# Attention's output differences in a tile of their own, and head 1's recurrence a few slots later

## The chip, the cores and the metric

The kernel runs on one core of one Trainium2 chip. The metric is device time in microseconds (us): the median of several runs of the whole program. Five engines with queues of their own work beside each other: TensorE (PE, matmuls), VectorE (DVE), ScalarE (ACT), GpSimd (POOL) and SyncE (SP, which here only issues DMA transfers). Each engine and each issuing queue works in order: an entry that waits holds up everything behind it on the same queue.

## The reference

One step of an encoder layer over 512 prompt and 32 sample frames with 2048 features, in float32. Heads of a gated recurrence (HGRN2) and heads of latent attention (MLA) run beside each other, their outputs are joined and projected, and a convolutional FFN follows:

```python
proj = x @ w_in
hq, hf, hi, hg, cq, ckv, kr = jnp.split(proj, SPLITS, axis=-1)
f = lb + (1.0 - lb) * jax.nn.sigmoid(hf)
o_h, s_new = hgrn2_recurrence(heads(hq), heads(1.0 - f), heads(jnp.log(f)), heads(hi), s0, blk)
...
o_a = mla_attention(q_nope, q_rope, k_nope, krs, v, q_pos, jnp.arange(past_len + T))
out = jnp.concatenate([o_h, o_a.reshape(B, T, D_MLA)], axis=-1) @ w_out
...
h = layer_norm(ALPHA * h + mix, ln1_g, ln1_b)
ff, conv_new = conv_ffn(h, conv_cache, w_up, w_gate, conv_w, conv_b, w_down)
h = layer_norm(ALPHA * h + ff, ln2_g, ln2_b)
```

There are 8 recurrent heads and 8 attention heads. `NI` is half of the 544 frames, 272.

## The kernel before

Each float32 operand is split into a high part (a copy by ACT, `wh`, `aH`) and a low part (a subtraction by DVE, `wl`, `aL`), and each product is made of three matmuls.

Most of the large projections are done by a divided product that needs 7 block products in place of 8. It works on sums and differences of the weight's four quarters and of the activations' quarters. `sums_of_inputs` forms these sums of the normalised input early and stores them in device memory (`si_dr`), using tiles of the attention's pool `mp` as rooms (the list `homes`). The sums come back as operands: s1 and s2 into a pool of their own (`smr`), s4 at the start of the next stage (`load_sum(gp, "s4")`, two loads at L738), s3 into the low halves of input tiles (`place_s3`, L781).

Sums of the later output projection's weights are formed by transfers alone: the list `forms` holds 32 of them (L93). The first 8 are issued by SP during the first projections. The other 24 are issued by POOL, two at a time, from `low` each time a divided product prepares its "s2" weights (L835). Groups c = 2 to 15 of divided products exist, two for each head from head 1 on. Stage 3 of the kernel, from about 767 us, reads the result.

Attention works on pairs of heads (`proj_pair`, `attend`). `attend(pr)` takes 9 items (query blocks). For each it makes scores, a softmax into a tile `p` (three slots, taken in turn, L603), transposes, and a product with the values, copied into the output tile `o` (L655, L651). At the end `o` is stored to `cat_dr` (L670), the difference of its two halves of frames is formed in place (L671, on POOL for pairs 0 to 2 and on DVE for pair 3), and the difference is stored to `d3_dr` (L672). Pair 3 runs beside the projection `head_ig(0)`, whose last step on DVE (L398) reads a PSUM tile that the next product needs.

The next stage opens the pool `gp` in the place of `mp`; a transfer into a `gp` tile waits for the last readers of whatever lay there. On PE, DVE and ACT its order is written out by hand, in slots. A divided group has 7 products in the order 11, s1, s2, s4, s3, 12, 22; each product has 24 matmuls (L889) and two slots, so a group has 14 slots and a head 28. At the middle of each product the result of the product before is taken out of PSUM (L874, L877), the weights of the product two further on get their low part (L831), and sums of raw weights are formed (L818, and L820 and L833 as adding transfers on POOL). Behind each slot's matmuls come steps of side work, given to slots by `beside_from(slot, generator, steps)`:

- `split_s4`: two steps, each an ACT copy (L742) and a DVE subtraction (L743) of half of s4. Its operands are first needed by the product s4, in slots 6 and 7.
- `split_s3`: four steps (L786, L787).
- `levels(h)`: the recurrence inside chunks. Step 0 makes Kp and Qp (L931, L932). Step 1 makes ten matmuls into the PSUM tile `sw` (L937), a masked copy (L938) and the first of seven levels. Each level is one set of matmuls (L954, L957, or L952 for the last) and DVE products of Qp and Kp (L958, L960), of totals (L966) and a masked copy (L970). The matmuls of a level need the products of the level before.
- `finish(h)`: 15 steps: transposes (L990), states (L1000, L1005 to L1014), outputs (L1022, L1024), their norm and gate, and the sums for the output projection, which read `cat_dr` and `d3_dr` through the tile `ab` (L983, L984).

`sw` has one buffer; the level matmuls and the state sums share two PSUM tiles in turn. Before, `levels(0)` takes slots 2 to 12, `finish(0)` 15 to 29, `levels(1)` 15 to 29, `finish(1)` 30 to 44, `levels(2)` 43 to 57. SP's and POOL's entries are put in order by a planner from the program order and its own estimate of what is ready.

Of the kernel before, what the change touches and what calls it, by code (L numbers as in the profile page):

```python
# [7 lines left out]
F32 = mybir.dt.float32  # L8
# [3 lines left out]
ALU = mybir.AluOpType  # L12
# [3 lines left out]
P = 128  # L16
# [4 lines left out]
T = TP + TS  # L21
PAST = 128
NK = TP + PAST + TS
HEADS = 8
# [18 lines left out]
NI = T // 2  # L43
# [12 lines left out]
N_PLAIN = 2  # L56
# [3 lines left out]
def tile_encoder_step(ctx, tc, xp, xs, w_in, w_in4, w_kr, w_q_b, w_kv_b, w_out, w_out4, w_up, w_gate, w_down, w_down2,  # L60
# [3 lines left out]
    V, A, G, PE = nc.vector, nc.scalar, nc.gpsimd, nc.tensor  # L64
    dma = nc.sync.dma_start
# [11 lines left out]
    d3_dr = [dram.tile([P, 2, NI], F32, name=f"d3d{k}", tag=f"d3d{k}") for k in range(HK // 2)]  # L77
# [19 lines left out]
    def form_next(n=0):  # L97
        if len(forms) > n:
            tc.keep_in_program_order(forms.pop(0)())
# [82 lines left out]
    def minus(out, a, b):  # L182
        V.tensor_tensor(out=out, in0=a, in1=b, op=ALU.subtract)

    def opposite(out, a, b):
        V.scalar_tensor_tensor(out=out, in0=a, scalar=-1.0, in1=b, op0=ALU.mult, op1=ALU.subtract)
# [215 lines left out]
    with tc.tile_pool(name="mp", bufs=1, side="right", reuse_waits="tile") as mp, tc.tile_pool(name="psa", bufs=4, space=PSUM) as psa:  # L402
# [17 lines left out]
        def a_tile():  # L420
            return psa.tile([P, 512], F32, name="at", tag="at")
# [48 lines left out]
        c = {}  # L470
# [140 lines left out]
        def attend(pr):  # L611
            qn, qr, kn, vt = pairs[pr]
            o = mp.tile([P, 2 * T], F32, name="o", tag="o").rearrange("p (j c) -> p j c", j=2)

            def scores(b, j):
                sc = a_tile()
                if b == 4:
                    for j, k in enumerate((kn[0], kn[1], krs)):
                        PE.matmul(sc[:, :160], qlast[pr % 2][:, j], k[:, TP:NK], start=j == 0, stop=j == 2)
                    return softmax(sc[:, :160], P, 160)  # L620
                nk = (b + 1) * P
                q0 = b * P
                PE.matmul(sc[:, :nk], qn[j][:, q0:q0 + P], kn[j][:, :nk], start=True, stop=False)
                for i, k in enumerate(c["kr"]):
                    PE.matmul(sc[:, :nk], qr[j][:, q0:q0 + P], k[:, :nk], start=False, stop=i == 1)
                V.tensor_tensor(out=sc[:64, q0 + 64:nk], in0=sc[:64, q0 + 64:nk], in1=amask, op=ALU.add)
                return softmax(sc[:, :nk], P, nk)

            def turn(b, p):
                tp = a_tile()  # L630
                t = mp.tile([P, T], F32, name="pT", tag="pT", bufs=3)
                if b == 4:
                    PE.transpose(tp[:, 0:P], p[:, 0:P], ident)
                    PE.transpose(tp[:, P:2 * P], p[:, 32:160], ident)
                    A.activation(plast[96:128, :], tp[96:128, P:P + 64], AF.Copy)
                    n = 64
                else:
                    n = (b + 1) * P
                    for k in range(b + 1):
                        PE.transpose(tp[:, k * P:(k + 1) * P], p[:, k * P:(k + 1) * P], ident)  # L640
                A.activation(t[:, :n], tp[:, :n], AF.Copy)
                return t

            def values(b, j, t):
                po = a_tile()
                if b == 4:
                    for j in range(2):
                        js = slice(j * 32, (j + 1) * 32)
                        PE.matmul(po[:, js], vt[:, 4, j, :], t[:, js], start=True, stop=False)
                        PE.matmul(po[:, js], vt[:, 5, j, :], plast[:, js], start=False, stop=True)  # L650
                    V.tensor_copy(o[:, :, TP:T], po[:, :64].rearrange("p (j c) -> p j c", j=2))  # L651
                    return
                for k in range(b + 1):
                    PE.matmul(po[:, :P], vt[:, k, j, :], t[:, k * P:(k + 1) * P], start=k == 0, stop=k == b)
                V.tensor_copy(o[:, j, b * P:(b + 1) * P], po[:, :P])  # L655

            items = [(b, j) for b in range(4) for j in range(2)] + [(4, 0)]
            n = len(items)
            ps, ts_ = {}, {}
            for i in range(n + 3):  # L660
                if i < n:
                    ps[i] = scores(*items[i])
                    yield
                if 0 <= i - 2 < n:
                    ts_[i - 2] = turn(items[i - 2][0], ps.pop(i - 2))
                    yield
                if 0 <= i - 3 < n:
                    values(*items[i - 3], ts_.pop(i - 3))
                    yield
            dma(cat_dr[4 + pr], o)  # L670
            (V if pr == 3 else G).tensor_tensor(out=o[:, :, :NI], in0=o[:, :, :NI], in1=o[:, :, NI:], op=ALU.subtract)  # L671
            dma(d3_dr[pr], o[:, :, :NI])  # L672

        ticks = [0]

# [4 lines left out]

        def sums_of_inputs():
            homes = [("p", T, 3)] * 3 + [("kn", NK, 2)] * 2 + [("pT", T, 3)] * 3
            homes += [(t, n, 1) for t, n in (("o", 2 * T), ("vt", 12 * P), ("qr0", 2 * T), ("qr1", 2 * T))]

            def room():
                for tag, n, bufs in homes:
                    t = mp.tile([P, n], F32, name=tag, tag=tag, bufs=bufs)
                    for i in range(n // T):
                        yield t[:, i * T:(i + 1) * T]

            rooms = room()
            rows = []
            for k in range(HK):
                rows.append((next(rooms), next(rooms)))
                for x, kg in zip(rows[k], (k, HK + k)):
                    dma(x, h0_dr[kg])
                if k % 2:
                    yield
            for k in range(HK):
                a, b = rows[k]  # L700
                t0, t1, t0b, t1b = (x[:, h] for x in (a, b) for h in H_)
                minus(t1b, t1b, t1)
                minus(t1, t0, t1)
                opposite(t0, t1b, t0)
                opposite(t0b, t0, t0b)
                for x, n in ((a, "a"), (b, "b")):
                    G.dma_start(si_dr[n][k // 4][:, k % 4], x.rearrange("p (w c) -> p w c", w=2))
                yield
# [55 lines left out]
    with tc.tile_pool(name="gp", bufs=1, side="right", reuse_waits="tile") as gp, tc.tile_pool(name="psg", bufs=1, space=PSUM) as psg:  # L764
# [37 lines left out]
        class Divided:  # L802
# [26 lines left out]
            def low(self, wh):  # L829
                wl = wp.tile([P, 1024], R, name="wl", tag="wl")  # L830
                V.tensor_tensor(out=wl, in0=self.t(self.key), in1=wh.bitcast(F32), op=ALU.subtract)  # L831
                if self.name == "s2":
                    G.dma_start(self.t("11"), self.src("21"), accum_op=ALU.add)  # L833
                    for _ in range(2):
                        form_next()  # L835
                elif self.name not in ("11", "s1"):
                    slots.append(self.raw.pop(self.key)[0])
                    supply()
                return wh, wl
# [21 lines left out]
        def settle():  # L861
            now, later[:] = later[:], []
            for f in now:
                f()
# [202 lines left out]
        with tc.manual_schedule(engines=MANUAL):  # L1067

            turns = {}

            def beside_from(slot, gen, steps):
                for n in steps:
                    turns.setdefault(slot + n, []).append(gen)

            def split_s4():
                for i in range(2):
                    split_sum("s4", i)
                    yield

            beside_from(1, split_s4(), (0, 2))  # L1080
            beside_from(4, split_s3(range(HK)), range(4))
            beside_from(0, levels(0), (2, 3, 5, 6, 7, 8, 9, 11, 12))
            beside_from(15, finish(0), range(15))
            for h in range(1, HEADS):
                s0 = 28 * (h - 1) + 15
                beside_from(s0, levels(h), (0, 2, 4, 6, 8, 10, 12, 13, 14) if h < HEADS - 1 else (0, 1, 3, 4, 6, 8, 9, 11, 12))
                if h < HEADS - 1:
                    beside_from(s0 + 15, finish(h), range(15))
            groups = [g for h in range(1, HEADS) for g in (divided_qf(h), divided_ig(h))]
            for slot, _ in enumerate(s for g in groups for s in g):  # L1090
                for gen in turns.pop(slot, ()):
                    next(gen, None)
            for _ in range(2):
                settle()
            for slot in sorted(turns):
                for gen in turns[slot]:
                    next(gen, None)
# [831 lines left out]
    with tc.manual_schedule():  # L1929
# [253 lines left out]
        class Last:  # L2183
            g, name, time = None, "11", 3.0
# [370 lines left out]
        _, rs = nrm.row_factor(ps)  # L2555
# [131 lines left out]
```

## Time and profile before

| what | value |
|---|---|
| median of 3 runs | 2342.21 us (2341.68 to 2342.52) |
| profiled execution | 2341.88 us, span 2340.1 us |
| PE busy | 2293.4 us, 98% of the span |
| DVE / ACT / POOL busy | 1724.8 / 1099.5 / 280.6 us |
| mean granted PE clock | 0.992 |
| DMA | 481.11 MB, mean 206 GB/s |

The profile is one execution. Its page gives busy times and the costliest groups; further views give the waits of an engine (who waited for whom), the rows of an engine in order of time, busy times with the granted clock in chosen stretches, and transfers with the time from issue to landing. `[0.82 <-ACT kn L584]` behind a row means that its engine sat idle for 0.82 us before it, until ACT's instruction of line 584 was done. `x24` is a count. Times in the rows are us from the start of the span. The attention pairs run from about 155 to 298 us, the hand-ordered stage follows to about 700 us.

### The profile page before, as it was taken

The numbers are of one execution on the slowest core, as the hardware profiler recorded it, in microseconds if no ns is written. First come the engines' busy times: TensorE is split into PE (matmuls) and PEld (weight loads), VectorE is DVE, ScalarE is ACT, GpSimd is POOL, SyncE is SP. The second block draws the span as 40 slices with busy tenths as digits, with TensorE's granted clock in tenths as the row PEclk, the third lists the DMA queues.
The fourth block names the chain that finished last, engine by engine and source line by source line (L and its number), as shares of the span: only waits on it lengthen the run. The fifth ranks groups of instructions, "written<-read, shape, count | busy, mean of one in ns | idle before, by whom it ended". The sixth has DMA issues, their size and how long they took to land.

```text
span 2340.1 us, 44591 instructions
## 1 busy us (share of the span) xinstructions
PE 2293.4 (98%) x18210; PEld 2276.8 (97%) x18210; DVE 1724.8 (74%) x2392; ACT 1099.5 (47%) x1684; POOL 280.6 (12%) x354
## 2 busy tenths in 40 slices
PE   7999989999999999999999999999999999999997
PEld 7999889999999999999999999999999999999997
DVE  7655657777777878987777777777777677777766
ACT  6344533444334537665455555555555433333324
POOL 1111101111101121000010000100001111111102
PEclk9999989999999999999999999999999999999998
DMA  7832356666766746777667667676676999889832
GB/s 265 294 112 89 113 141 154 173 173 187 173 178 225 264 162 206 215 209 201 206 176 230 179 187 220 169 226 187 182 224 185 365 324 312 257 276 308 291 107 79
DMA packets 176189, 481.11 MB, mean 206 GB/s; under 512 B 15984, under 2 KB 78192, under 8 KB 168560
## 3 DMA queue, kind: packets, MB, share of 16 engines
q1 hardware_dynamic: 138928, 320.76, 39.3%
q0 software_dynamic: 37056, 157.50, 29.1%
q8 instruction: 143, 2.34, 0.4%
q14 instruction: 62, 0.51, 0.1%
HBM read 398.69 MB, written 93.57 MB: 210 GB/s over the span
## 4 chain that ended last, share of the span: by engine, by line
PE 64%; ACT 1%; DVE 1%; issue 0%; ACTq 0%; DVEq 0%
PE main L1349 22%; PE acc L1349 17%; PE main L1380 11%; PE acc L1380 7%; PE acc L148 3%; PE main L148 1%; PE main L1834 1%; PE sb L1834 1%; ACT y L2435 0%; ACT wh L1290 0%; PE main L1162 0%; ACT zb L1490 0%; PE main L1157 0%; ACT za L1490 0%; PE acc L1157 0%
## 5 line engine op out<-in xcount | busy, mean ns | idle before, releaser
L1291 DVE TENSOR_TENSOR wl<-raw,wh 128x1024 fp32r<-128x1024 f32 x371 | 456.4, 1230 | 192.4 <-ACT wh L1290 192.1
L1290 ACT ACTIVATE wh<-raw 128x1024 fp32r<-128x1024 f32 x371 | 392.2, 1059 | 410.2 <-PE main L1349 99.3
L1349 PE MATMUL main<-op,wh 128*128 128x272 f32 x1408 | 265.4, 288 | 0.0
L1349 PE MATMUL acc<-ops,wh 128*128 128x272 f32 x1344 | 254.1, 288 | 0.0
L1349 PE MATMUL main<-ops,wh 128*128 128x272 f32 x1344 | 254.1, 288 | 0.0
L1349 PEld LDWEIGHTS main<-op,wh 128*128 128x128 f32 x1408 | 221.1, 188 | 0.0
L1349 PEld LDWEIGHTS acc<-ops,wh 128*128 128x128 f32 x1344 | 211.2, 188 | 0.0
L1349 PEld LDWEIGHTS main<-ops,wh 128*128 128x128 f32 x1344 | 211.1, 188 | 0.0
L1349 PE MATMUL main<-op,wl 128*128 128x272 f32 x704 | 203.1, 289 | 0.3 <-DVE wl L1291 0.3
L1349 PE MATMUL main<-ops,wl 128*128 128x272 f32 x672 | 193.9, 289 | 0.0
L1349 PE MATMUL acc<-ops,wl 128*128 128x272 f32 x672 | 193.9, 288 | 0.0
L1349 PE MATMUL acc<-op,wh 128*128 128x272 f32 x832 | 157.5, 288 | 1.0 <-ACT ea L1675 1.0
L1290 ACT ACTIVATE wh<-rawl 128x1024 fp32r<-128x1024 f32 x93 | 98.8, 1063 | 116.7 <-PE acc L1349 39.9
L831 DVE TENSOR_TENSOR wl<-raw,wh 128x1024 fp32r<-128x1024 f32 x98 | 120.4, 1229 | 43.6 <-ACT wh L826 42.5
L889 PE MATMUL main<-s,wh 128*128 128x272 f32 x672 | 135.9, 299 | 2.5 <-DVE hproj L398 2.5
L889 PE MATMUL main<-aH,wh 128*128 128x272 f32 x448 | 133.4, 298 | 0.0
L1291 DVE TENSOR_TENSOR wl<-rawl,wh 128x1024 fp32r<-128x1024 f32 x93 | 113.8, 1224 | 26.3 <-ACT wh L1290 26.2
L1349 PEld LDWEIGHTS main<-op,wl 128*128 128x128 f32 x704 | 132.4, 188 | 0.5 <-DVE wl L1291 0.5
L1349 PEld LDWEIGHTS acc<-op,wh 128*128 128x128 f32 x832 | 130.5, 188 | 1.2 <-ACT ea L1675 1.2
L826 ACT ACTIVATE wh<-raw 128x1024 fp32r<-128x1024 f32 x98 | 103.4, 1055 | 59.4 <-DVE raw L818 58.0
L889 PE MATMUL main<-aH,wl 128*128 128x272 f32 x448 | 129.5, 289 | 0.0
L889 PE MATMUL main<-aL,wh 128*128 128x272 f32 x448 | 129.0, 288 | 0.0
(542 smaller groups left out, 6182.4 us busy)
## 6 DMA issues: line engine op xcount, KB each, us to landing
raw<-in_w_in SPq DMA_DIRECT2D x76, 512.0 KB, 5.7
raw<-in_w_up SPq DMA_DIRECT2D x71, 512.0 KB, 4.9
raw<-in_w_gate SPq DMA_DIRECT2D x71, 512.0 KB, 4.9
raw<-in_w_down SPq DMA_DIRECT2D x67, 512.0 KB, 9.2
opd<-ohl SPq DMA_DIRECT2D x20, 1088.0 KB, 5.5
ops<-opd POOLq DMA_DIRECT2D x20, 1088.0 KB, 11.9
raw<-in_w_up POOLq DMA_DIRECT2D x35, 512.0 KB, 5.2
opd<-ohl SPq DMA_DIRECT2D x20, 816.0 KB, 6.4
```

The costliest lines, as they stand in the source:

```text
L148: PE.matmul(ps, ww[:, wcols[0]:wcols[1]], aa[:, hs[j]], start=first and i == 0, stop=last and i == 2, skip_group_check=True)
L826: A.activation(wh, self.t(self.key), AF.Copy)
L831: V.tensor_tensor(out=wl, in0=self.t(self.key), in1=wh.bitcast(F32), op=ALU.subtract)
L889: PE.matmul(out, ww[:, k * P:(k + 1) * P], aa, start=name in ("11", "s1", "12") and k == 0 and q == 0, stop=k == HK - 1 and q == 2, skip_g ...
L1290: A.activation(wh, src, AF.Copy)
L1291: V.tensor_tensor(out=wl, in0=src, in1=wh.bitcast(F32), op=ALU.subtract)
L1349: PE.matmul(ps, ww[:, k * P:(k + 1) * P], aa, start=self.first and k == 0 and i == 0, stop=k == n - 1 and i == 2, skip_group_check=True)
L1380: PE.matmul(banks[:, 512 * u:512 * u + NI], ww[:, (u * n + k) * P:(u * n + k + 1) * P], aa, start=self.first and k == 0 and i == 0, stop=k ...
L1834: PE.matmul(self.bank, ww[:, k * P:(k + 1) * P], aa, start=self.first and k == 0 and i == 0, stop=k == HK - 1 and i == 2, skip_group_check ...
```

## The change

- The difference of the output's halves is written to a tile with the tag `p`, and that tile is stored; `o` is only read.
- In the list of rooms `o` comes last, so that in the pool it lies behind `vt`, `qr0` and `qr1`. The sums of inputs take their rooms in the new order.
- The first divided group (c = 2) issues no weight-sum transfer; the groups c = 3 to 14 issue the 24.
- `split_s4` has slots 3 and 4, not 1 and 3. `levels(1)` has slots 18 to 33, not 15 to 29, and `finish(1)` 34 to 48, not 30 to 44.

```diff
             dma(cat_dr[4 + pr], o)
-            (V if pr == 3 else G).tensor_tensor(out=o[:, :, :NI], in0=o[:, :, :NI], in1=o[:, :, NI:], op=ALU.subtract)
-            dma(d3_dr[pr], o[:, :, :NI])
+            d = mp.tile([P, T], F32, name="p", tag="p", bufs=3).rearrange("p (j c) -> p j c", j=2)
+            (V if pr == 3 else G).tensor_tensor(out=d, in0=o[:, :, :NI], in1=o[:, :, NI:], op=ALU.subtract)
+            dma(d3_dr[pr], d)
...
-            homes += [(t, n, 1) for t, n in (("o", 2 * T), ("vt", 12 * P), ("qr0", 2 * T), ("qr1", 2 * T))]
+            homes += [(t, n, 1) for t, n in (("vt", 12 * P), ("qr0", 2 * T), ("qr1", 2 * T), ("o", 2 * T))]
...
-                    for _ in range(2):
+                    for _ in range(2 if self.c > N_PLAIN else 0):
                         form_next()
...
-            beside_from(1, split_s4(), (0, 2))
+            beside_from(3, split_s4(), range(2))
...
                 s0 = 28 * (h - 1) + 15
-                beside_from(s0, levels(h), (0, 2, 4, 6, 8, 10, 12, 13, 14) if h < HEADS - 1 else (0, 1, 3, 4, 6, 8, 9, 11, 12))
+                beside_from(s0, levels(h), (3, 5, 7, 9, 11, 13, 15, 17, 18) if h == 1 else
+                            (0, 2, 4, 6, 8, 10, 12, 13, 14) if h < HEADS - 1 else (0, 1, 3, 4, 6, 8, 9, 11, 12))
                 if h < HEADS - 1:
-                    beside_from(s0 + 15, finish(h), range(15))
+                    beside_from(s0 + (19 if h == 1 else 15), finish(h), range(15))
```

## The prediction

> **What bounds the kernel now.** I read the page's busy shares first, then the waits of TensorE (PE), then stretches around those waits, and last the rows of the engines and queues inside them. The page:
>
> ```profile
> span 2340.1 us, 44591 instructions
> PE 2293.4 (98%) x18210; PEld 2276.8 (97%) x18210; DVE 1724.8 (74%) x2392; ACT 1099.5 (47%) x1684; POOL 280.6 (12%) x354
> ```
>
> PE is busy 98% of the span, so an edit of other engines can only win where PE stands still or runs at a reduced clock. Such places lie around 300 to 313, 349 to 357 and near 380 us, where head 0's and head 1's recurrences start. The waits of PE there, in three stretches (waited for, us in total, times, longest):
>
> ```profile
> PE sw L937 <- DVE Kp L931: 5.4, 1, 5.4
> PE main L889 <- DVE hproj L398: 2.5, 1, 2.5
> ...
> PE s L954 <- DVE S L1007: 1.3, 1, 1.3
> PE sw L937 <- ACT vT L995: 0.8, 1, 0.8
> ...
> PE s L952 <- DVE tot L966: 0.8, 1, 0.8
> ```
>
> A second price shows in stretches of the same instructions. Columns: stretch, us, PE busy, PEld, DVE, ACT, POOL, granted clock, DMA share, GB/s.
>
> ```profile
> 344.65:347.76 3.11, 3.11 (x28) 3.11 (x26) 1.52 (x3) 2.32 (x4) 1.80 (x2) 1.00 0.47 63
> 303.50:308.31 4.81, 4.80 (x24) 4.58 (x24) 0.00 (x0) 0.00 (x0) 0.00 (x0) 0.65 1.06 262
> 358.34:362.96 4.62, 4.62 (x26) 4.62 (x26) 2.74 (x5) 0.00 (x0) 0.00 (x0) 0.63 0.69 123
> 300.96:328.13 27.17, 19.14 (x113) 18.72 (x113) 15.31 (x28) 9.41 (x17) 2.09 (x4) 0.75 0.54 157
> ```
>
> The first three are each one block product (24 matmuls). At clock 1.00 it takes 3.11 us; behind the 2.5 us wait it takes 4.81 and behind the 1.3 us wait 4.62. So a wait of 1.3 us or more also costs 1.5 to 1.7 us of clock. The fourth stretch runs from the end of product 11 to head 0's fourth level: clock 0.75, PE busy 19.14 of 27.17 us.
>
> Who holds PE there? DVE rows, then ACT, then SP's queue (start us, us, engine, line, operation):
>
> ```profile
> 294.88 0.23 DVE L651 COPY o<-at 128x64 f32<-128x64 f32 x1 [2.03 <-PE at L650]
> 302.09 0.73 DVE L671 TENSOR_TENSOR o<-o 128x544 f32<-128x544 f32 x1 [6.99 <-DMA catd<-o]
> 302.74 0.71 DVE L398 TENSOR_TENSOR hproj<-hproj,main 128x544 f32<-128x544 f32 x1
> 310.85 1.29 DVE L743 TENSOR_TENSOR s<-s 128x1088 fp32r<-128x1088 f32 x1 [7.40 <-ACT s L742]
> ...
> 297.97 0.62 ACT L397 ACTIVATE hproj<-main 128x544 f32<-128x544 f32 x1 [1.98 <-PE main L148]
> 309.71 1.11 ACT L742 ACTIVATE s<-s 128x1088 fp32r<-128x1088 f32 x1 [11.11 <-DMA s<-sib]
> ...
> 295.14 0.32 SPq L670 DMA_DIRECT2D catd<-o  x1
> 302.85 0.57 SPq L672 DMA_DIRECT2D d3d<-o  x1
> 303.52 1.27 SPq L738 DMA_DIRECT2D s<-sib  x2
> ```
>
> One chain: the last attention pair's output is complete at 295.1. L671 subtracts in place, so DVE waits 6.99 us until the store of `o` has read it. L398 stands behind it on DVE and frees the PSUM tile of product s1: the 2.5 us wait. On SP the difference's store waits for L671, and the two loads of sum s4 stand behind that store, issued at 303.52. ACT waits 11.11 us for them, then DVE splits them ahead of Kp (L931): the 5.4 us wait.
>
> **The change part by part: the difference tile.** L671 writes another tile and no longer waits for the store of `o`. It runs at 295.1 to 295.9, and L398 as soon as L397 is done (298.6) to 299.3; PE needs it at 300.96. The 2.5 us wait and its clock loss go.
>
> What is late next is the load of s4. The new tile takes the tag `p`, three slots used in turn. Up to the last pair that is 3 homes + 3 x 10 + 9 = 42 takes, so pair 3 gets the first slot again. In the memory plan of the kernel before that slot is bytes 173920 to 176096, and s4's first half is loaded into 173088 to 177440. So the first s4 load cannot start before the difference's store has read its tile: a new wait, at the head of SP's queue, with s4's other load, the mask `hm`, raw weights, `s0` and `ab` behind it. The DMA view and the time from issue to landing (min/median/max):
>
> ```profile
> wf1s<-in_w_out POOLq DMA_DIRECT2D x2, 512.0 KB, 7.6
> catd<-o SPq DMA_DIRECT2D x1, 544.0 KB, 6.9
> ...
> L672 SPq DMA_DIRECT2D d3d<-o x4: 567/572/600, 194.6 to 302.8; - x4
> DMA to landing us min/median/max: 3.2/3.8/5.3
> ...
> L738 SPq DMA_DIRECT2D s<-sib x4: 562/608/653, 255.3 to 304.1; - x4
> DMA to landing us min/median/max: 4.7/6.0/7.0
> ```
>
> The difference's store is issued at 295.9. The two weight-sum transfers of this stretch (7.6 us each) are gone, so I take 3.4 us for it, between minimum and median, and 5.3 us for s4: landing at 304.6. The ends are 295.9 + 3.2 + 4.7 = 303.8 and 295.9 + 5.3 + 7.0 = 308.2.
>
> **The split of s4, slots 3 and 4.** Its first half now stands behind Kp and Qp, so Kp waits only for L398 and one weight split: done by 302, needed at about 304. The 5.4 us wait goes. But both halves now lie between head 0's first and second levels. The rows I add up, DVE first and then PE:
>
> ```profile
> 316.12 0.76 DVE L938 COPY_PREDICATED attnT<-hm,sw 128x544 f32<-128x544 uint8 x1 [0.66 <-issue]
> 318.17 0.44 DVE L958 TENSOR_TENSOR Qp<-Qp,hproj 128x272 f32<-128x272 f32 x1 [1.29 <-PE s L957]
> 319.79 1.27 DVE L831 TENSOR_TENSOR wl<-raw,wh 128x1024 fp32r<-128x1024 f32 x1
> 320.96 1.49 DVE L787 TENSOR_TENSOR aL<-aL,aH 128x272 fp32r<-128x272 f32 x4
> ...
> 322.62 1.00 PE L954 MATMUL s<-Qp,Kp 128*128 128x64 f32 x8
> ...
> 349.26 1.30 PE L937 MATMUL sw<-hproj,Kp 128*128 128x128 f32 x10 [0.79 <-ACT vT L995]
> ```
>
> From s4's landing to the operands of level 3: ACT split 1.1, DVE split 1.3, L938 0.8, level 1 1.6 (318.17 to 319.79), L831 1.2, second split 1.3, four L787 1.5, two products of level 2 0.8: 9.6 us, so 314.2. PE gets there at 300.96 + 3.11 (s1) + 1.3 (L937) + 1.0 + 3.11 (s2) + 1.0 + 1.55 (half of s4) = 312.0. New wait: 2.2 us, plus 1.6 us of clock, 3.8 in all. Before, the stretch to the fourth level took 27.17 us for 3 x 3.11 + 1.3 + 3 x 1.0 = 13.6 us of work, a loss of 13.6. Gain 13.6 - 3.8 = 9.8. Ends: with landing at 308.2 DVE is ready at 317.8, 5.8 us late in two waits, each with 1.6 of clock: loss 9.0, gain 4.6. If s4 lands early enough, L938 can still not start before PE has done L937 (305.4): ready 305.4 + 0.8 + 1.6 + 1.2 + 1.3 + 1.5 + 0.8 = 312.6, a wait of 0.6 without a clock drop, gain 13.0.
>
> [...]
>
> **Head 1's levels and finish, three and four slots later.** Its first level no longer shares a slot with head 0's state sums, whose PSUM tiles L954 waits for (1.3 us, then 1.5 of clock); L937 no longer follows head 0's transpose (0.8); and the last two levels stand two slots apart, not one (0.8). Together 4.4. It is still done before its tiles are taken again (head 3's projections, slot 56 on). In exchange head 1's finish now overlaps head 2's levels in slots 43 to 48, where DVE has about as much work as PE. Bounds of a new wait: 0, and 1.3 + 1.5 = 2.8 like the worst one removed. I take 0.8, the row of the crowded place near 380. Gain 3.6.
>
> **The weight-sum transfers, one group later.** POOL issues the same 24 transfers; the first two leave the crowded stretch (counted above), the others move one group (about 28 us). Last issue and first reading, before:
>
> ```profile
> L93 POOL DMA_DIRECT2D wf<-in_w_out x4: 893/1083/1300, 605.1 to 643.0; - x4
> ...
> L1278 SPq DMA_DIRECT2D xr<-wf1s x2: 394/420/447, 766.7 to 767.2; - x2
> ```
>
> 643 + 28 = 671 leaves 96 us: cost 0. If that cover went, the reader would wait on a transfer, 7.6 us by the row above.
>
> **The output tile's place.** Where `o` lay, `tot` and `ab` of the next stage come to lie; now it is `vt`, last read by the matmuls before 294.88. The sums of inputs use the same tiles in another order. Cost 0, PE has no wait on them.
>
> **The first three pairs.** The difference there runs on POOL and its tile comes out of the same three `p` slots, so the next pair's third softmax must wait until the difference's store has read it. SP, ACT and POOL rows of the first and third pair:
>
> ```profile
> 188.92 0.33 SPq L670 DMA_DIRECT2D catd<-o  x1
> 254.83 0.33 SPq L670 DMA_DIRECT2D catd<-o  x1
> ...
> 196.25 0.47 ACT L606 ACTIVATE p<-at,mx 128x256 f32<-128x256 f32 x1 [0.65 <-DVE mx L605]
> 262.92 0.46 ACT L606 ACTIVATE p<-at,mx 128x256 f32<-128x256 f32 x1
> ...
> L671 POOL TENSOR_TENSOR o<-o x3: 1373/1733/2277, 191.8 to 258.1; 128x544 f32<-128x544 f32 x3
> ```
>
> Landing: 188.9 + 1.7 + 3.8 = 194.4 against 196.25, and 254.8 + 2.3 + 3.8 = 260.9 against 262.92. Slack about 1.9 us, so 0. It is kept only if SP issues the store at once.
>
> **Sum.** 9.8 + 3.6 = 13.4 us. Profiled execution: 2341.88 us (span 2340.1); its median of runs, 2342.21, is 0.3 higher. 2341.9 - 13.4 + 0.3 = 2328.8, forecast 2329. Later stages have PE as busy, so the gain is carried to the end.
>
> **Rivals.** (1) The wait only changes its name: s4's load behind the store lands at the late end. Gain 4.6 + 3.6 = 8.2: 2334. For it: SP's order. Against it: the lighter DMA. (2) Head 1's new places give nothing, because DVE was the limit there and slots 43 to 48 stall: 2329 + 3.6 = 2333. (3) Slower: SP issues the differences' stores of the first three pairs behind an entry that waits itself, and ACT, in order, stops at the third softmax with the weight copies behind it. One such wait in this trace:
>
> ```profile
> SPq L781 <- PE main L148: 11.2, 6, 7.4
> ```
>
> With 7.4 us of delay each pair waits 7.4 - 1.9 = 5.5 us and 1.5 of clock: 3 x 7.0 = 21, less the 13.4: about 2350. It ends slower once the delay passes 4.9 us (3 x (4.9 - 1.9) + 4.5 = 13.5). Against it: most of SP's entries there do not wait, and PE has projection products to run meanwhile.
>
> **How the numbers follow.** Forecast 0.62 (its own range 2325.5 to 2332), rival 1 0.17, rival 2 0.10, rival 3 0.05, others 0.06. Low: gains 13.0 and 4.4, 2325. High: 4.6 and 4.4 - 2.8 = 1.6, 2336, and 1 us for a partial rival 3: 2337. A difference of 0.2% (4.7 us) is about what a measurement can tell. Faster by more: forecast, rivals 1 and 2 less a little, 0.85; within 0.2%: 0.09; slower: 0.06.
>
> **What would show it.** L671 right behind L651 with no wait on `catd`; no PE wait on L398; s4's loads issued at 299 to 300 and landed near 305; L937 with no wait on L931, but a PE wait of about 2 us on L958 or L960 near 312; no waits of PE on L1007, L995 and L966 for head 1. Wrong if s4 is issued at 303 or later, if PE waits in slots 43 to 48, or if the attention pairs show waits on `p`.

## The result and the profile after

The change makes the kernel faster: 2326.82 us (median of 4 runs, 2325.28 to 2327.92) against 2342.36 us (4 runs, 2341.68 to 2343.48), a ratio of 0.9933 with a 95% interval of 0.9916 to 0.9950. That is 15.5 us. The forecast was 2329 us, 13.4 us less than the profiled execution before.

The page of the kernel after (engine, busy us, share of the span, instructions):

```profile
span 2325.6 us, 44592 instructions
PE 2287.8 (98%) x18210; PEld 2271.3 (98%) x18210; DVE 1722.3 (74%) x2392; ACT 1100.2 (47%) x1684; POOL 280.0 (12%) x354
```

The matmuls are the same 18210; PE's share does not move. The span is 14.5 us shorter, and PE's busy time 5.6 us, with a mean granted clock of 0.996 where it was 0.992. Where the time came from is read at the places where PE stood still before. From L671 on, a line has a number higher by one than before (L672 is the difference, L673 its store, L739 the loads of s4). The waits of PE between 296 and 330 us (waited for, us in total, times, longest):

```profile
PE main L890 <- DVE hproj L398: 0.8, 1, 0.8
PE s L955 <- DVE Kp L961: 0.6, 1, 0.6
PE s L955 <- DVE tot L967: 0.5, 1, 0.5
```

Before there were 5.4 us (on Kp) and 2.5 us (on L398). Between 330 and 420 us a single wait of 0.3 us is left, where head 1 had 1.3, 0.8 and 0.8. The rows behind these waits, as before DVE first, then ACT, then SP's queue (start us, us, engine, line, operation):

```profile
293.85 0.23 DVE L651 COPY o<-at 128x64 f32<-128x64 f32 x1 [2.02 <-PE at L650]
294.11 0.72 DVE L672 TENSOR_TENSOR p<-o 128x544 f32<-128x544 f32 x1
...
299.91 0.71 DVE L398 TENSOR_TENSOR hproj<-hproj,main 128x544 f32<-128x544 f32 x1
...
296.69 1.06 ACT L827 ACTIVATE wh<-raw 128x1024 fp32r<-128x1024 f32 x1 [3.03 <-PE main L148]
297.76 1.28 ACT L397 ACT_TABLE_LOAD   x1
299.06 0.62 ACT L397 ACTIVATE hproj<-main 128x544 f32<-128x544 f32 x1
302.58 1.11 ACT L743 ACTIVATE s<-s 128x1088 fp32r<-128x1088 f32 x1 [2.21 <-DMA s<-sib]
...
294.10 0.32 SPq L670 DMA_DIRECT2D catd<-o  x1
294.86 0.32 SPq L673 DMA_DIRECT2D d3d<-p  x1
298.20 1.21 SPq L739 DMA_DIRECT2D s<-sib  x2
```

The difference starts right behind the last copy, without the 6.99 us wait; s4's loads are issued at 298.20 where they were at 303.52, and ACT begins their split at 302.58, not 309.71. One line of the transfers' view (issued between 285 and 325 us; count, KB, us to landing) has moved as well, though nothing about this transfer was edited:

```profile
catd<-o SPq DMA_DIRECT2D x1, 544.0 KB, 2.7
```

It was 6.9 us before. The experiments turn on this line.

**Where the 14.5 us came from.** The same instruction in both traces gives the gain up to that place. Attention's last copy (L651) starts at 294.88 before and 293.85 after: 1.03 us. Head 0's fourth level (the end of the prediction's 27.17 us stretch) starts at

```profile
328.13 1.08 PE L954 MATMUL s<-Qp,Kp 128*128 128x64 f32 x8
```

before, and after at

```profile
315.89 1.08 PE L955 MATMUL s<-Qp,Kp 128*128 128x64 f32 x8 [0.48 <-DVE tot L967]
```

a gain of 12.24 us, so 11.2 in this stretch. Behind the last head's finish the rows are, before and then after,

```profile
735.99 0.75 DVE L1045 SCALAR_TENSOR_TENSOR og<-sw,par,hproj 128x512 f32<-128x512 f32 x1 [2.96 <-PE sw L1043]
```

```profile
719.30 0.75 DVE L1046 SCALAR_TENSOR_TENSOR og<-sw,par,hproj 128x512 f32<-128x512 f32 x1 [2.96 <-PE sw L1044]
```

16.7 us, of which head 1 brings the last 4.5. Behind that about 2.2 us are given back (16.7 against 14.5 at the end).

### The profile page after: what moved, and what is told of

It is laid out like the page before. It is cut to its first block, busy times and chain, and to the rows that moved or that the text cites. A ratio compares the mean times of both kernels' runs of the same rounds, so it can differ in the third digit from the quotient of the medians.

```text
span 2325.6 us, 44592 instructions
## 1 busy us (share of the span) xinstructions
PE 2287.8 (98%) x18210; PEld 2271.3 (98%) x18210; DVE 1722.3 (74%) x2392; ACT 1100.2 (47%) x1684; POOL 280.0 (12%) x354
## 4 chain that ended last, share of the span: by engine, by line
PE 88%; issue 4%; DVE 3%; DMA 2%; ACT 2%; POOL 0%; ACTq 0%; DVEq 0%; SPq 0%; POOLq 0%
PE main L1351 22%; PE acc L1351 17%; PE main L890 12%; PE main L148 9%; PE main L1382 8%; PE acc L1382 6%; PE acc L148 3%; PE s L955 2%; PE main L1836 1%; PE sb L1836 1%; PE main L593 1%; PE at L654 1%; PE at L623 1%; DMA xr<-wf1s 1%; PE sb L148 1%
## 5 line engine op out<-in xcount | busy, mean ns | idle before, releaser
L1293 DVE TENSOR_TENSOR wl<-rawl,wh 128x1024 fp32r<-128x1024 f32 x93 | 113.8, 1224 | 26.8 <-ACT wh L1292 26.7
```

The lines of the kernel that those rows point to most:

```text
L1293: V.tensor_tensor(out=wl, in0=src, in1=wh.bitcast(F32), op=ALU.subtract)
```

## The experiments

The prediction ascribed the chain's removal to the difference tile, and took the two weight-sum transfers out of the stretch as a help to the landing time only. The rival theory, once the store of `o` was seen to land in 2.7 us, is that the transfers were what made that store, and everything behind it, late. In the expectations the first is called the queue theory, the second the traffic theory. In the table "saved" is the ratio's distance from 1 times 2343 us, and beside it what the profiled execution's span is below 2340.1 us. The executions of one kernel differ by up to 5.0 us (two weight sums back: 2330.95 to 2335.95), so both are given. The kernels were timed on different occasions, each against the kernel before on the same chip.

| kernel | median us | ratio (95%) | saved by ratio | saved in span |
|---|---|---|---|---|
| the change | 2326.82 | 0.9933 (0.9916 to 0.9950) | 15.7 | 14.5 |
| tile alone | 2341.37 | 0.9992 (0.9982 to 1.0001) | 1.9 | 0.8 |
| no weight sums in the first group, alone | 2336.57 | 0.9971 (0.9961 to 0.9981) | 6.8 | 5.8 |
| change, difference in place | 2328.44 | 0.9942 (0.9927 to 0.9957) | 13.6 | 14.2 |
| change, two weight sums back | 2332.99 | 0.9955 (0.9938 to 0.9971) | 10.5 | 5.9 |
| change, one weight sum back | 2331.46 | 0.9948 (0.9933 to 0.9963) | 12.2 | 11.0 |
| change, split of s4 in its old slots | 2332.31 | 0.9951 (0.9936 to 0.9966) | 11.5 | 10.0 |
| change, head 1 in its old slots | 2330.77 | 0.9946 (0.9929 to 0.9962) | 12.7 | 10.4 |
| change, pair 3's difference elsewhere | 2326.62 | 0.9930 (0.9916 to 0.9945) | 16.4 | 16.2 |
| the same, head 0's levels later | 2325.93 | 0.9927 (0.9912 to 0.9942) | 17.1 | 16.2 |
| the same, last levels later too | 2326.41 | 0.9928 (0.9912 to 0.9945) | 16.9 | 16.5 |

The two single edits (tile alone, no weight sums alone) stand apart from each other and from the change beyond their intervals. The intervals of the kernels with one part undone all overlap the change's: there the verdict rests on the trace rows, and the medians only agree in sign.

**The tile alone.** The kernel before with the first hunk of the change and nothing else:

```diff
-            (V if pr == 3 else G).tensor_tensor(out=o[:, :, :NI], ...)
-            dma(d3_dr[pr], o[:, :, :NI])
+            d = mp.tile([P, T], F32, name="p", tag="p", bufs=3).rearrange(...)
+            (V if pr == 3 else G).tensor_tensor(out=d, ...)
+            dma(d3_dr[pr], d)
```

> The kernel before with the difference tile alone; the first group's weight sums, the places of s4's split and head 1's slots stay as before. Queue theory (DVE and SP stood behind the in-place difference): L671's place has no wait on the store of o, the 2.5 us wait of PE on L398 goes; but the split of s4 still stands ahead of Kp, and with the weight sums on the wire s4 lands near 306, so PE still waits some 5 us for Kp: 2337 (gain 5). Traffic theory (the two weight-sum transfers made the stores and loads slow, the in-place wait only shows it): gain below 2, 2341.

Ratio 0.9992: next to nothing, with an interval that holds 1. Transfers, SP's row of s4's loads, and PE's longest wait in this kernel:

```profile
catd<-o SPq DMA_DIRECT2D x1, 544.0 KB, 8.5
d3d<-p SPq DMA_DIRECT2D x1, 272.0 KB, 8.4
...
303.71 1.21 SPq L739 DMA_DIRECT2D s<-sib  x2
...
PE sw L938 <- DVE Kp L932: 9.5, 1, 9.5
```

The wait on L398 is gone as forecast. But the difference's store, issued early, needs 8.4 us to land, not the 3.2 to 5.3 of the rows before, and s4's loads, behind it on SP, are issued at 303.71, as late as without the tile (303.52). What PE no longer waits on L398 it waits on Kp: 9.5 us, where the queue theory expected some 5.

**The weight sums alone.** The kernel before, but the first group issues none:

```diff
-                    for _ in range(2):
+                    for _ in range(2 if self.c > N_PLAIN else 0):
                         form_next()
```

> The kernel before without the first group's weight-sum transfers, nothing else changed. Traffic theory: the store of o takes about 3 us, not 6.9, so the in-place difference runs near 298, s4 is issued near 299.5 and lands near 304.3, PE waits about 4 us for Kp: 2335 (gain 7). Queue theory: the wait is in the order, and shorter transfers give 1 to 2 us: 2341.

Ratio 0.9971. Transfers, the difference's row on DVE, and PE's wait:

```profile
catd<-o SPq DMA_DIRECT2D x1, 544.0 KB, 2.7
d3d<-o SPq DMA_DIRECT2D x1, 272.0 KB, 2.7
...
298.72 0.73 DVE L671 TENSOR_TENSOR o<-o 128x544 f32<-128x544 f32 x1 [2.81 <-DMA catd<-o]
...
PE sw L937 <- DVE Kp L931: 3.6, 1, 3.6
```

With the in-place subtraction left as it was, its wait falls from 6.99 to 2.81 us, s4's loads are issued 3.4 us earlier (300.15) and the 5.4 us wait of PE becomes 3.6. The 2.5 us wait of PE on L398 is gone here too, without the tile: L398 starts at 299.43, not at 302.74. So the chain was long because the stores were slow, not because the subtraction was in place.

**The change without the tile.** Everything else kept, the new order of the rooms too:

```diff
-            d = mp.tile([P, T], F32, name="p", tag="p", bufs=3).rearrange(...)
-            (V if pr == 3 else G).tensor_tensor(out=d, ...)
-            dma(d3_dr[pr], d)
+            (V if pr == 3 else G).tensor_tensor(out=o[:, :, :NI], ...)
+            dma(d3_dr[pr], o[:, :, :NI])
```

> The changed kernel with the difference formed in place again, all else as changed. Traffic theory: the store of o now takes 2.7 us, the difference runs near 297, s4's loads need not wait for the difference's store to land (its tile is not under them) and are issued near 298, as with the tile: 2326 to 2328, no difference. Queue theory: DVE and SP stand behind the store again, s4 lands 3 us or more later: 2331 or more.

2328.44 us, a ratio that overlaps the change's, and a span longer by 0.3 us. DVE's difference, SP's loads of s4 and PE's wait before the third level, and then two stretches around this wait (stretch, us, PE, PEld, DVE, ACT, POOL busy, granted clock, DMA share, GB/s):

```profile
298.30 0.73 DVE L671 TENSOR_TENSOR o<-o 128x544 f32<-128x544 f32 x1 [2.89 <-DMA catd<-o]
300.80 1.20 SPq L738 DMA_DIRECT2D s<-sib  x2
315.12 1.08 PE L954 MATMUL s<-Qp,Kp 128*128 128x64 f32 x8 [2.06 <-DVE Kp L960]
...
310.77:314.19 3.42, 2.30 (x19) 2.08 (x18) 3.42 (x7) 2.98 (x7) 0.00 (x0) 1.00 0.38 116
314.19:317.60 3.41, 2.48 (x21) 2.51 (x22) 3.41 (x9) 0.00 (x0) 0.00 (x0) 1.00 0.09 37
```

The wait on the store of `o` is back at 2.89 us and s4 comes 2.6 us later; PE then waits 2.06 us where the change has 0.64, and the clock stays at 1.00 in both stretches and behind them, up to 370 us. The time is close to what the traffic theory gave (2326 to 2328), but its step was wrong: it had s4's loads issued near 298, as with the tile. Without the slow stores the tile is worth at most a couple of us.

**The weight sums back.** The change with the two transfers in the first group again:

```diff
-                    for _ in range(2 if self.c > N_PLAIN else 0):
+                    for _ in range(2):
```

> The changed kernel with the first group's weight-sum transfers back, all else as changed. Traffic theory: the difference's store takes about 5 us and s4 about 6, s4 lands near 306 and PE waits 3 to 4 us before level 3 with a clock drop: 2331. Queue theory: the tile is enough, 2327 to 2328.

2332.99 us (2330.95 to 2335.95; the profiled execution is the slowest of them, 2335.95). Transfers, and PE's row at the wait, before the second level:

```profile
catd<-o SPq DMA_DIRECT2D x1, 544.0 KB, 8.3
d3d<-p SPq DMA_DIRECT2D x1, 272.0 KB, 8.1
...
wf1s<-in_w_out POOLq DMA_DIRECT2D x2, 512.0 KB, 7.8
...
312.29 1.97 PE L955 MATMUL s<-Qp,Kp 128*128 128x64 f32 x8 [2.83 <-DVE Kp L961]
```

s4's loads are issued at 303.26 and their split starts at 308.45. Then the stretch between two changes of the clock (columns as above):

```profile
311.83:328.90 17.07, 16.36 (x73) 16.07 (x74) 13.05 (x29) 6.68 (x14) 0.00 (x0) 0.50 0.34 95
```

A 2.83 us wait is followed by 17.07 us at half clock, which can cost up to 8.5 us by estimate (half of the stretch). Here the price lies in the clock more than in the wait. The median of the four runs is 3 us below this one, so the others may have lost less.

**One weight sum back.** The two transfers of the first group both add a weight quarter to what already lies in device memory, each to a target of its own. Does it take both?

```diff
-                    for _ in range(2 if self.c > N_PLAIN else 0):
+                    for _ in range(2 if self.c > N_PLAIN else 1):
```

> The changed kernel with one weight-sum transfer in the first group instead of none or two. If the first of the two (issued near 291, beside the store of o and of the difference) does the harm: those stores still take about 8 us, s4 is issued near 303 and lands near 308, PE waits 2 to 3 us before level 3: 2331 to 2333, as with two. Rival (the second, issued near 300.5 beside s4's loads): s4 lands near 303 to 304, 2327 to 2328.

Transfers, and then two stretches around PE's wait (columns as above):

```profile
wf1s<-in_w_out POOLq DMA_DIRECT2D x1, 512.0 KB, 9.4
catd<-o SPq DMA_DIRECT2D x1, 544.0 KB, 8.5
d3d<-p SPq DMA_DIRECT2D x1, 272.0 KB, 8.2
...
308.03:311.45 3.42, 1.42 (x12) 1.20 (x11) 2.93 (x5) 3.42 (x7) 0.00 (x0) 1.00 1.04 397
311.45:321.69 10.24, 9.89 (x44) 9.60 (x45) 9.70 (x21) 3.99 (x9) 0.00 (x0) 0.50 0.44 139
```

No: one adding transfer alone lands in 9.4 us and slows the two stores just as two do. s4's loads are issued at 303.13, and PE waits 2.0 us before head 0's second level (309.31 to 311.31, in the first of the two stretches), with half the clock for 10.24 us behind it. The time, 2331.46, is what was expected of one such transfer doing the harm.

**The split of s4 in its old slots.**

```diff
-            beside_from(3, split_s4(), range(2))
+            beside_from(1, split_s4(), (0, 2))
```

> The changed kernel with the split of s4 in slots 1 and 3 again. By the prediction's steps: s4 lands at 302.6, its first half is split on DVE ahead of the weight split and of Kp, so Kp is ready near 302.6 + 1.1 + 1.3 + 1.2 + 0.4 = 306.6, PE waits 2.5 to 3 us on L931 after s1 with a clock drop of 1.6, and the waits before the later levels go: 2329 (2 to 3.5 slower than the change). Rival (the place of the split costs nothing, the work only changes places on DVE): 2327.

PE's wait, and two stretches:

```profile
PE sw L938 <- DVE Kp L932: 3.1, 1, 3.1
...
305.00:310.00 5.00, 3.87 (x18) 3.87 (x19) 3.67 (x5) 3.94 (x8) 0.00 (x0) 0.52 0.60 172
310.00:315.00 5.00, 5.00 (x24) 5.00 (x24) 4.27 (x9) 0.00 (x0) 0.00 (x0) 0.50 0.10 10
```

The split stands ahead of Kp again: 3.1 us of wait, and 10 us at half clock, where 1.6 us of clock loss had been expected. The median is 5.5 us above the change's (4.2 us by the ratios) and the span 4.5. The split's slots are a part of the gain of their own, of a size like the weight sums'.

**Head 1 in its old slots.** The old tuples of `levels(1)`, and `finish(1)` at `s0 + 15`:

```diff
-                beside_from(s0, levels(h), (3, 5, 7, 9, 11, 13, 15, 17, 18) if h == 1 else
-                            (0, 2, 4, 6, 8, 10, 12, 13, 14) if h < HEADS - 1 else (...))
+                beside_from(s0, levels(h), (0, 2, 4, 6, 8, 10, 12, 13, 14) if h < HEADS - 1 else (...))
-                    beside_from(s0 + (19 if h == 1 else 15), finish(h), range(15))
+                    beside_from(s0 + 15, finish(h), range(15))
```

> The changed kernel with head 1's levels and finish in the slots of before. If the four us come from the slots: the waits of PE on L1007, L995 and L966 are back with the clock drop behind the 1.3 us one, 2331 (4.5 slower). Rival (those waits came from the backlog that the late s4 left on DVE and are gone anyway): 2327.

The three waits of PE are back, one for one:

```profile
PE s L955 <- DVE S L1008: 1.3, 1, 1.3
PE sw L938 <- ACT vT L996: 0.8, 1, 0.8
PE s L953 <- DVE tot L967: 0.8, 1, 0.8
```

The granted clock between 345 and 350 us is 0.68. After head 1 this kernel is 4.5 us behind the change (the same instruction at 673.52 against 669.00), and the median is 4.0 us higher (3.0 us by the ratios).

**Pair 3's difference out of s4's way.** In the change, s4's first load must wait until the difference's store has read its tile. Here pair 3 takes a slot of the tag `pT` for it:

```diff
+            tag = "pT" if pr == 3 else "p"
-            d = mp.tile([P, T], F32, name="p", tag="p", bufs=3).rearrange(...)
+            d = mp.tile([P, T], F32, name=tag, tag=tag, bufs=3).rearrange(...)
```

> The changed kernel with pair 3's difference in a slot of the tag pT, which lies under Kp and Qp of the next stage and not under s4. s4's loads need not wait for the difference's store: issued near 295.5, landed near 300. If that new wait set the remaining stops: the split runs at once and PE's waits before the second to fourth level (0.3, 0.6 and 0.5 us) shrink to what DVE's work alone makes, about 0.6 in all: 2326 (gain 1 or less). Rival (DVE's work alone makes them): no change of these waits.

```profile
295.87 1.30 SPq L740 DMA_DIRECT2D s<-sib  x2
...
301.87 1.11 ACT L744 ACTIVATE s<-s 128x1088 fp32r<-128x1088 f32 x1 [0.92 <-DMA s<-sib]
```

The loads are issued 2.33 us earlier, but land in 6.4 us, not 4.7, so ACT gains 0.71 us. PE's waits before the third and fourth level stay at 0.6 and 0.5 us: DVE's own work makes them, and the wait of s4's load in the change costs nothing that shows. The time, 2326.62, can't be told from the change's.

**Head 0's levels later**, on top of the last kernel, in two versions:

```diff
-            beside_from(0, levels(0), (2, 3, 5, 6, 7, 8, 9, 11, 12))
+            beside_from(0, levels(0), (2, 3, 5, 7, 8, 9, 10, 11, 12))
```

> As d_apart, and head 0's third to sixth level one slot later (slots 7 to 11 in place of 6 to 9), so that DVE has one slot more for s4 and s3. If DVE's work between the first and the third level makes the rest of the waits: no wait of PE on the levels, 2325.5 (gain 1 to 1.5). Rival: the waits move to a later level, or the sixth and seventh level, which now stand one slot apart, wait: 2327.

The 0.6 us wait before the third level went, the one before the fourth stayed (0.57 us), and one came before the seventh level, whose predecessor now stood a single slot ahead: 0.8 us, on the totals of L968.

2325.93 us. With the tuple's end at `10, 12, 13` in place of `10, 11, 12`:

> As d_apart, with head 0's third to sixth level in slots 7 to 10 and the seventh in slot 12, step 9 in slot 13: two slots again between the sixth and the seventh level. The 0.8 us wait of PE on L968 ahead of the seventh level goes, the 0.6 and 0.3 us ones before the third stay: 2325 (under 1 us better than d_apart, less than the measurement tells; the waits are the test). Rival: another wait of 0.5 to 1 us takes its place.

That wait went as well; left are 0.8 us on L398, 0.6 us before head 0's fourth level and 0.3 us before one of head 1's. The time is 2326.41 us: the three last kernels and the change can't be told apart, as what is left to win here is under 2 us. The new place of `o` among the rooms was not tried alone.

## Why the prediction was right, and where its steps were not

The sign, the time (2326.8 in 2325 to 2337, inside the forecast's own range) and most of the profile's signs came as said. That the total is only 1.1 us off (13.4 forecast, 14.5 in the span) is in part luck: three terms came out 1.4, 0.9 and 1.0 us larger than forecast, and 2.2 us of the gain were lost again further on. What held up and what did not, in its own order:

- **The difference tile as the cause: wrong.** The prediction read DVE's row `[6.99 <-DMA catd<-o]` as a fault of the queue's order, cured by another tile. The tile alone saved 0.8 to 1.9 us. The row ahead of it, `catd<-o` landing in 6.9 us beside two `wf1s<-in_w_out` of 7.6 us, held the cause: the weight-sum transfers slowed the stores. The four stores of `o` in the trace before say so, in a row that the prediction did not use:

```profile
L670 SPq DMA_DIRECT2D catd<-o x4: 320/327/332, 188.9 to 295.1; - x4
...
DMA to landing us min/median/max: 2.7/2.9/6.9
```

  The slow one is the exception. The step that failed is the cause given for the 6.99 us wait: the prediction gave the removal of this wait and of the 2.5 us one to the tile, and used the absence of the weight sums only to choose the landing time of the difference's store, 3.4 us. That size held (3.3 us in the change). But without the weight sums the 2.5 us wait is gone from the in-place kernel as well, and with them the tile does not bring s4 forward: the difference's store then takes 8.1 to 8.4 us, beyond the late end of 5.3. The sum came out because the change does both.
- **L398.** Forecast: no wait, L398 at 298.6. It ran at 299.91 and PE waited 0.84 us. ACT took a weight copy and a table load of 1.28 us before L397, and DVE had a weight split and Kp and Qp ahead of L398. The order of the rows of before was taken over, and the moved split of s4 changed it: with the split in its old slots L397 runs at 297.06, and the wait is not there.
- **s4 and the third and fourth levels.** Forecast: issue at 299.3, landing at 304.6, a wait of 2.2 us with 1.6 of clock. Measured: issue 298.20, split from 302.58, and waits of 0.64 and 0.48 us without a clock drop. This is the mis-sized term: 9.8 us forecast, 11.2 measured. It lies between the forecast and the early end that the prediction gave (13.0, a 0.6 us wait); what misses to 13.0 is mostly the 0.84 and 0.48 us.
- **Head 1.** Forecast 3.6 with a new wait of 0.8 us; measured 4.5, and slots 43 to 48 have no wait of PE. The lower bound of that term (no new wait, 4.4) was the right one.
- **The attention pairs.** Forecast 0; 1.03 us came out of them. SP's and ACT's rows behind pair 2, before and then after:

```profile
261.12 1.22 SPq L738 DMA_DIRECT2D s<-sia  x2
...
266.50 1.11 ACT L742 ACTIVATE s<-s 128x1088 fp32r<-128x1088 f32 x1 [2.87 <-DMA s<-sia]
```

```profile
258.34 1.35 SPq L739 DMA_DIRECT2D s<-sia  x2
...
264.76 1.11 ACT L743 ACTIVATE s<-s 128x1088 fp32r<-128x1088 f32 x1
```

The difference of pair 2 does not wait for the store of `o` there either, so its store is issued at 256.38, not 260.38, the next loads on SP come 2.78 us earlier, and ACT no longer waits 2.87 us for them. Between 240 and 296 us PE waits 1.7 to 1.8 us in the three traces with the in-place difference and 0.5 to 1.0 us in the nine with the tile. The prediction looked for harm in these pairs and not for a gain.

- **The rivals.** Rival 1, s4 landing at the late end, is what the kernels with one or two weight sums back show (issue at 303.1 and 303.3): the price was right in kind, and the place was the transfers. Rival 2 and rival 3 did not occur: POOL forms its three differences at 188.96, 222.10 and 254.98 us, right behind the pairs' last copies and without a wait on a store, and ACT has no wait on `p` tiles held by a store.
- **Carried to the end: not quite.** 16.7 us at 719 us became 14.5 at the end. The other profiled executions gave back between nothing (pair 3's difference elsewhere) and 1.8 us (head 1 in its old slots). About 0.7 us of it is one wait of PE near 790 us, on ACT's tile `n_e`: 1.3 us in the change and with head 1 in its old slots, 0.6 us before. The rest was not followed and stays open.

## What to carry to other kernels

When an engine waits for a transfer, compare its landing time with that of the same transfer elsewhere in the trace, before the order of the queue is blamed: here it was 6.9 against 2.7 us, and a transfer on another queue was the reason. Test the parts of a change alone as well as undone, because two cures of one wait hide each other: either edit alone removed the 2.5 us wait, but the tile alone left s4 as late as before and won almost nothing, and on top of the other edit little was left for it to win. A wait of PE was priced here by the clock behind it, not by its length: 2.06 us of wait had no stretch at half clock behind them, 2.83 us had 17.07 us.

## What the runs showed of the hardware that was not expected

**A transfer that occupies the DMA engines and moves little.** The first group's weight-sum transfers go from device memory to device memory and add there. The stretch from 295 to 300 us, first of the kernel before, then of the change, and then with one such transfer back (last columns: granted clock, DMA share, GB/s):

```profile
295.00:300.00 5.00, 5.00 (x42) 5.00 (x41) 0.11 (x1) 1.62 (x2) 0.00 (x0) 1.00 1.06 182
```

```profile
295.00:300.00 5.00, 4.93 (x40) 4.71 (x38) 2.22 (x4) 3.00 (x4) 0.00 (x0) 1.00 0.51 173
```

```profile
295.00:300.00 5.00, 4.95 (x40) 4.72 (x38) 2.21 (x4) 2.99 (x4) 0.00 (x0) 1.00 1.04 223
```

With them the 16 engines are occupied throughout at 182 to 223 GB/s; without them half, at 173 GB/s. Between 285 and 325 us of the kernel before, the queue of POOL's transfers takes 26.7% of the engines' time for 1.57 MB, and SP's 29.9% for 4.21 MB. The stores beside them take two to three times as long (544 KB: 2.7 and 2.8 us without, 6.9 to 8.5 with; 272 KB: 2.6 to 3.4 us without, 5.3 in the kernel before and 8.1 to 8.4 where the store is issued earlier). How the engines divide their time was not measured.

**The price of a wait in clock.** The half-clock stretches in these traces last 3.4 us (after 1.3 us of wait, head 1 in its old slots), 6.8 us (after 3.6 us, no weight sums, alone), 10.2 us (after 2.0 us, one weight sum back; and after 3.1 us, split in its old slots), 13.7 us (beside 9.5 us, tile alone) and 17.1 us (after 2.8 us, two weight sums back): one to five times 3.4 us. The wait of 2.06 us in the kernel with the in-place difference cost no clock at all. So the length of the wait does not set the price. Estimated as at most half of the stretch at half clock, it was 0 behind 2.06 us, up to 5.1 us behind 2.0 us, up to 8.5 us behind 2.8 us, and behind 9.5 us less than that, as PE was busy for only 6.9 of the 13.7 us. The prediction's 1.5 to 1.7 us behind each wait of 1.3 us or more is the smallest of these steps; in the kernel before, 10.2 us at half clock lie around the end of the 5.4 us wait.

What sets it, no run here shows. Two waits of nearly the same length stand against each other: behind the 2.06 us with the in-place difference the clock is 1.00 up to 370 us, behind the 2.0 us with one weight sum back it is 0.50 from 311.45 to 321.69 us. Nor do the runs show why the clock stays low while PE is never idle: with two weight sums back PE is busy for all 5.00 us from 320 to 325 us, at 0.50.
